# Written order on ScalarE and VectorE, and the product G2-G3 moved behind M7, in a two-layer GLA and retention trunk

## The chip, the cores and the metric

The kernel runs on one core of a Trainium2 chip. The metric is the device time of one execution in microseconds (us). The median of three runs stands for a kernel; one execution is also recorded by the hardware profiler, and all rows below come from that one.

A core has five engines, each with its own instruction queue worked off in order: TensorE (PE; matmuls, its weight loads are listed as PEld), ScalarE (ACT), VectorE (DVE), GpSimd (POOL) and SyncE (SP, which here only issues transfers). Sixteen DMA engines move data between HBM and the on-chip memory SBUF; matmuls write to PSUM.

## What is computed

The reference is a decoder trunk of two layers on 256 tokens of width 2048, in float32: one layer of gated linear attention (GLA, 4 heads) and one of retention (8 heads), each with RMSNorm before it, a SiLU gate, an output projection and a residual add, and a last RMSNorm.

```python
def gla_mixer(h, w_in, ...):           # retention_mixer has the same frame
    q, k, v, gate = split(h @ w_in)    # k-dimension 2048
    o = chunked_attention(q, k, v, decay)
    return (norm(o) * silu(gate)) @ w_out

for i in range(2):
    h = h + mixer_i(rms_norm(h, g_i))
return rms_norm(h, final_norm)
```

Nearly all the work is the products with `w_in` and `w_out`, all in float32 accuracy: every float32 block is split into a high part `hi` (rounded to what the fast matmul format holds) and a rest `lo`, and three matmuls (high with high, high with low, low with high) stand for one.

## The kernel before, in words

**Blocks.** The weights are cut into blocks of 256 rows of the k-dimension by 512 columns. A block lies in SBUF as a tile of 128 partitions by 1024 numbers (512 KB), which holds two k-tiles. A group of 512 output columns takes 8 blocks. `_plan` (L56) writes two lists: `loads`, the blocks to be fetched in order, and `subs`, the blocks to be split in order (576 of them).

**Split.** `emit_split` (L226) takes the next entry of `subs`: ScalarE copies the block to `hi` (L238), VectorE subtracts to get `lo` (L239). `hi` and `lo` have 4 buffers each, plain blocks (`raw`) 4 as well. `next_weights` (L263) keeps the splits 3 entries ahead of the one that TensorE is about to use (`LOOK = 3`); plain loads are issued from the SP queue 3 loads ahead of the splits (`DMA_LOOK = 3`).

**A pair.** `pair` (L310) makes one group of value columns V and one group of gate columns G together, 16 times in all: 8 times in the GLA layer (tile names `ga_...`) and 8 times in the retention layer (`re_...`). Blocks G4 to G7 and V4 to V7 are used plainly (`normal`, L338: 12 matmuls, both token halves). For blocks 0 to 3 of both, a 2x2 scheme of Winograd's kind takes 7 products where 8 would be needed (`product`, L330: two blocks, 12 matmuls of 512 columns over one token half or over a sum of halves). Its weight sums are formed in place: after a block G0, G1, V2 or V3 was split, GpSimd issues a transfer that adds the next block to it in SBUF (L245, `accum_op=ALU.add`), and the sum is split again. In this document G0' is the block G0 after the first addition (G0+V0), G0'' after the second (+V2), G0''' after the third (+G2); G1 goes with it, and V2', V3' are V2+V0 and V3+V1. So each of G0 and G1 passes a chain of three rounds: split, transfer, split, transfer, split, transfer, split.

**Order of TensorE in a pair, before.** G0-G1 | V4 | V2-V3 | V5 | G0'-G1' | V6 | G2-G3 | first half of V7 | G0''-G1'' | second half of V7 | V2'-V3' (this product is called M7) | G4 | G0'''-G1''' | G5 | G6 | G7. This order is fixed on TensorE: `wmm` stamps each matmul with one token, and instructions of one engine that carry it keep their written order. On ScalarE and VectorE there was no such stamp: a scheduler orders them by priority (written order, unless `high_priority` lifts an instruction) and by its own simulated times.

**Copies and joins.** The 7 products share PSUM banks, so intermediate sums are copied out by ScalarE (`keepf`, L358 to L360): `sg[0]` from bank g1 after G0-G1, `o[1]` from bank g0 after G0'-G1', `o[0]` from g1 after G0''-G1'', and `sg[1]` from g1 after M7. The next matmul that writes the bank waits for the copy. After M7, the next one that writes g1 is the second half of G4: 6 matmuls lie between. VectorE joins the pieces (L389 to L393, L402), `v_split` (L656) scales and splits V, and `g_silu` (L667) applies SiLU at the end of the pair.

**Beside the pairs.** Small steps of attention (`side`) are advanced one after each product or block: rotation, scores, decay, transposes. Each head begins with a group of query and key columns (`group_w`, 8 blocks), and after every 2 GLA heads or 4 retention heads comes a half of the output projection (`out_half`).

Of the kernel before, what the change touches and what calls it, by code (L numbers as in the profile page):

```python
# [10 lines left out]
F32 = mybir.dt.float32  # L11
# [3 lines left out]
AF = mybir.ActivationFunctionType  # L15
ALU = mybir.AluOpType
# [39 lines left out]
def _plan():  # L56


    loads, subs, last = [], [], {}

    def load(gid, j, tag="raw"):
        last[gid, j] = len(loads)
        loads.append((gid, j, tag))

    def use(gid, js, add=None):
        for j in js:
            subs.append((last[gid, j], None if add is None else (add[0], add[1] + j % 2)))

    def plain(gid, js=range(NSUB)):
        for j in js:  # L70
            load(gid, j, "xz"[j // 2] if not subs and j < 4 else "raw")
            use(gid, [j])

    def pair(g, v):
        def fresh(gid, js, tag="raw"):
            for j in js:
                load(gid, j, tag)
            use(gid, js)

        fresh(g, (0, 1), "x")  # L80
        fresh(v, (4,))
        fresh(v, (2, 3), "z")
        fresh(v, (5,))
        use(g, (0, 1), (v, 0))
        fresh(v, (6,))
        fresh(g, (2, 3))
        fresh(v, (7,))
        use(g, (0, 1), (v, 2))
        use(v, (2, 3), (v, 0))
        fresh(g, (4,))  # L90
        use(g, (0, 1), (g, 2))
        fresh(g, (5,))
        fresh(g, (6,))
        fresh(g, (7,))

    def gla(h):
        plain(("aqk", h))
        for g in (2 * h, 2 * h + 1):
            pair(("ag", g), ("av", g))

    def ret(h):
        plain(("rqk", h))
        pair(("rg", h), ("rv", h))

    def out_half(name, half):
        cut = READY[name]
        for js in (range(cut), range(cut, NSUB)):
            for c in range(2):
                plain((name, half, c), js)
        for c in (2, 3):  # L110
            plain((name, half, c))

    for half in range(2):
        for h in (2 * half, 2 * half + 1):
            gla(h)
# [13 lines left out]
def kernel(  # L129
# [17 lines left out]
    nc = tc.nc  # L147
# [19 lines left out]
    mm = nc.tensor.matmul  # L167
    keep = tc.keep_in_program_order

    def wmm(*args, **kw):  # L170
        tc.stamp_issue_order_token(nc.tensor.matmul(*args, **kw).ins, "weights")  # L171


    def const(shape, name, dtype=F32):
# [51 lines left out]
    def emit_split(pieces=1):  # L226
        i = emitted["sub"]
        if i >= len(subs):
            return
        c = subs[i][0]  # L230
        while emitted["raw"] <= min(c + DMA_LOOK, len(loads) - 1):
            emit_raw()
        src = raws[c]
        hi, lo = split_tiles(i)
        step = SUB // pieces
        for k in range(pieces):
            sl = slice(k * step, (k + 1) * step)
            nc.scalar.activation(hi[:, sl], src[:, sl], AF.Copy)  # L238
            nc.vector.tensor_tensor(lo[:, sl], src[:, sl], hi[:, sl].bitcast(F32), ALU.subtract)  # L239
        splits[i] = (hi, lo)  # L240
        emitted["sub"] += 1
        later[c].popleft()
        if later[c]:
            more = w_all[places[later[c][0]]].rearrange("p (k n) -> p k n", n=GW)
            nc.gpsimd.dma_start(src, more, accum_op=ALU.add)  # L245
# [64 lines left out]
    def pair(lhs, name, on_v, on_g, hook):  # L310
# [3 lines left out]
        v = v_p.tile([P, 2, 2, GW], F32R, tag="v", name=f"{name}_v")  # L314
        sg = sg_p.tile([P, 2, GW], F32, tag="sg", name=f"{name}_sg")
        o = o_p.tile([P, 2, GW], F32, tag="o", name=f"{name}_o")
        g1, v0, v1, g0 = acc(4, f"{name}_ps")
# [12 lines left out]
        def product(ps, left, stop=False):  # L330
            for j in range(2):
                hi, lo = next_weights()
                for q in range(SUB):
                    k = j * SUB + q
                    three(ps, left(k, 0), left(k, 1), hi, lo, q, stop and k == QK - 1)
            advance()

        def normal(p0, p1, j, stop=False, halves=False):  # L338
            hi, lo = next_weights()

            def half(t):
                for q in range(SUB):
                    kt = j * SUB + q
                    cols = slice(t * P, (t + 1) * P)
                    three((p0, p1)[t], lhs[:, kt, 0, cols], lhs[:, kt, 1, cols], hi, lo, q, stop and q == SUB - 1)
                if t:
                    advance()

            half(0)
            if halves:  # L350
                return lambda: half(1)
            half(1)

        plain = lambda kt0, t: lambda k, a: lhs[:, kt0 + k, a, t * P : (t + 1) * P]
        summed = lambda i: lambda k, a: s[:, i, k, a, :]
        tt = nc.vector.tensor_tensor

        def keepf(dst, ps):  # L358
            with tc.high_priority():
                nc.scalar.activation(dst, ps, AF.Copy)  # L360

        product(g1, plain(0, 0), stop=True)
        keepf(sg[:, 0, :], g1)
# [2 lines left out]
        hook(1)  # L366
        product(v0, summed(0))
        hook(2)
        normal(v0, v1, 5)
        hook(3)  # L370
        product(g0, summed(1), stop=True)
        keepf(o[:, 1, :], g0)
        begun.discard(id(g0))
        closed.discard(id(g0))
        hook(4)
        normal(v0, v1, 6)
        hook(5)
        product(g0, plain(4, 0))
        hook(6)
        second = normal(v0, v1, 7, stop=True, halves=True)  # L380
        product(g1, summed(2), stop=True)
        keepf(o[:, 0, :], g1)
        second()
        product(g1, summed(3), stop=True)
        keepf(sg[:, 1, :], g1)
        hook(7)
        normal(g0, g1, 4)
        hook(8)
# [9 lines left out]
        normal(g0, g1, 6)  # L398
        hook(11)
        normal(g0, g1, 7, stop=True)  # L400
        with tc.high_priority():
            tt(sg[:, 0, :], g0, sg[:, 0, :], ALU.add)  # L402
            on_g(sg, [sg[:, 0, :], g1])
        return sg

    def make_sums(lhs, name):
# [249 lines left out]
    def v_split(r2):  # L656
        def run(v, o):
            for t in range(2):
                x, sc = o[:, t, :], r2[:, t : t + 1]
                nc.scalar.activation(v[:, t, 0, :], x, AF.Copy, scale=sc)  # L660
                nc.vector.scalar_tensor_tensor(
                    v[:, t, 1, :], x, sc, v[:, t, 0, :].bitcast(F32), ALU.mult, ALU.subtract
                )

        return run

    def g_silu(r):  # L667
        def run(sg, src):
            for t in range(2):
                keep(nc.scalar.activation(sg[:, t, :], src[t], AF.Silu, scale=r[:, t : t + 1]))  # L670

        return run

# [585 lines left out]
```

## Time and profile before

| What | Value |
|---|---|
| Median of 3 runs | 1492.73 us (1484.79 to 1494.83) |
| The profiled execution | 1495.53 us |
| Its span, first to last instruction | 1493.8 us |
| TensorE busy | 1423.0 us (95%), 6608 matmuls |
| VectorE busy | 1063.3 us (71%) |
| ScalarE busy | 844.1 us (57%) |
| GpSimd busy | 175.2 us (12%) |
| TensorE clock granted, mean | 0.978 of full speed |
| DMA | 340.21 MB, mean 228 GB/s |

How to read the rows: in the list of waits a row names the waiting engine, the tile and line of its instruction, after the arrow who ended the wait, then the total in us, the number of waits and the longest. In a timeline a row has the start and the length in us, engine, line, operation, tiles as out<-in with their shapes, and in brackets the idle time of the engine before it and what ended it. In a table of stretches each engine has its busy time with the number of instructions; then come the granted share of the TensorE clock, the DMA engines' mean busy share and GB/s. An x count in a table of one line counts that line's instructions alone. A matmul's length overlaps the next one's; what counts is the distance of their starts.

### The profile page before, as it was taken

What the parts mean: (1) busy time and instruction counts of PE and PEld (TensorE: products, weight loads), DVE (VectorE), ACT (ScalarE), POOL (GpSimd) and SP (SyncE); (2) the same over time, 40 slices, a digit from 0 to 9 for tenths busy, and PEclk for the clock granted to TensorE, in tenths of its full rate; (3) what the DMA queues carried; (4) which work ended last, traced back from release to release, by engine and by line L of the source; (5) the groups of instructions that cost most, each with busy time, mean ns of one, the idle gap of its engine ahead of it and who ended that gap; (6) DMA issues with size and microseconds to landing.
All of it is one profiled execution on the core that took longest, in us unless ns stands there. A gap on an engine that the chain in (4) does not pass through costs nothing. (4 is left out here: it accounts for less than half of the span.)

```text
span 1493.8 us, 18563 instructions
## 1 busy us (share of the span) xinstructions
PE 1423.0 (95%) x6608; PEld 1160.4 (78%) x6608; DVE 1063.3 (71%) x1602; ACT 844.1 (57%) x1135; POOL 175.2 (12%) x237
## 2 busy tenths in 40 slices
PE   8898998999998999999999899989999999999997
PEld 6677876888876878788878787868888777787887
DVE  8689688854896696666767777766547676768664
ACT  4676675653575566554656565654335555656553
POOL 1111213000140032000111111110002010101000
PEclk9999998999999999999999999999999999999999
DMA  9997699556989689755996969696579697969663
GB/s 314 307 237 223 163 257 250 204 187 197 291 241 259 169 233 226 278 172 181 280 270 172 268 173 275 170 318 194 187 256 269 218 233 219 249 191 234 236 199 111
DMA packets 90332, 340.21 MB, mean 228 GB/s; under 512 B 10416, under 2 KB 10928, under 8 KB 88832
## 3 DMA queue, kind: packets, MB, share of 16 engines
q1 hardware_dynamic: 67344, 240.81, 46.7%
q0 software_dynamic: 22176, 97.14, 30.2%
q8 instruction: 52, 0.85, 0.2%
q10 hardware_dynamic: 720, 1.09, 0.2%
q14 instruction: 40, 0.33, 0.1%
HBM read 326.41 MB, written 12.58 MB: 227 GB/s over the span
## 5 line engine op out<-in xcount | busy, mean ns | idle before, releaser
L239 DVE TENSOR_TENSOR lo<-raw_raw,hi 128x1024 fp32r<-128x1024 f32 x375 | 459.4, 1228 | 241.4 <-ACT hi L238 238.6
L238 ACT ACTIVATE hi<-raw_raw 128x1024 fp32r<-128x1024 f32 x375 | 396.0, 1057 | 359.9 <-PE ga_ps L171 76.0
L171 PE MATMUL re_ps<-hi,xhl 128*128 128x512 f32 x704 | 236.6, 407 | 24.9 <-ACT re_sg L360 24.9
L171 PE MATMUL ga_ps<-hi,xhl 128*128 128x512 f32 x704 | 240.2, 412 | 15.5 <-ACT ga_sg L360 13.0
L238 ACT ACTIVATE hi<-raw_x 128x1024 fp32r<-128x1024 f32 (+1 forms) x130 | 136.0, 1052 | 166.5 <-DMA raw_x<-in_w_all 98.2
L239 DVE TENSOR_TENSOR lo<-raw_x,hi 128x1024 fp32r<-128x1024 f32 (+1 forms) x130 | 157.0, 1217 | 101.0 <-ACT hi L238 98.2
L171 PEld LDWEIGHTS re_ps<-hi,xhl 128*128 128x128 f32 x704 | 137.1, 195 | 60.3 <-ACT re_sg L360 28.4
L171 PE MATMUL rqk_ps<-xhl,hi 128*128 128x512 f32 x512 | 179.7, 393 | 1.5 <-ACT re_sg L670 1.5
L171 PEld LDWEIGHTS ga_ps<-hi,xhl 128*128 128x128 f32 x704 | 138.6, 197 | 51.9 <-ACT ga_sg L360 16.4
L171 PE MATMUL ga_ps<-lo,xhl 128*128 128x512 f32 x352 | 146.1, 415 | 2.8 <-DVE lo L239 2.6
L171 PE MATMUL re_ps<-lo,xhl 128*128 128x512 f32 x352 | 143.3, 407 | 0.0
L171 PE MATMUL rqk_ps<-xhl,lo 128*128 128x256 f32 x512 | 140.3, 283 | 0.0
L245 POOL DMA_DIRECT2D raw_x<-in_w_all x96 | 83.3, 868 | 347.9 <-DVE lo L239 315.2
L171 PEld LDWEIGHTS rqk_ps<-xhl,hi 128*128 128x128 f32 x512 | 94.9, 188 | 21.4 <-ACT re_sg L670 3.4
L171 PEld LDWEIGHTS rqk_ps<-xhl,lo 128*128 128x128 f32 x512 | 96.7, 189 | 2.5
L171 PE MATMUL gqk_ps<-xhl,hi 128*128 128x512 f32 x256 | 92.3, 402 | 0.8 <-ACT ga_sg L670 0.6
L171 PE MATMUL ga_ps<-hi,sums_a 128*128 128x512 f32 x256 | 85.9, 394 | 1.4 <-ACT ga_o L360 0.9
L171 PEld LDWEIGHTS ga_ps<-lo,xhl 128*128 128x128 f32 x352 | 69.5, 197 | 22.2 <-DVE lo L239 6.7
L171 PE MATMUL re_ps<-hi,sums_r 128*128 128x512 f32 x256 | 85.2, 392 | 0.3 <-ACT hi L238 0.2
L239 DVE TENSOR_TENSOR lo<-raw_z,hi 128x1024 fp32r<-128x1024 f32 x64 | 77.2, 1223 | 9.2 <-ACT hi L238 9.0
L171 PE MATMUL gb_ps<-hi,ogt 128*128 128x512 f32 x256 | 81.9, 397 | 0.0
L171 PE MATMUL ra_ps<-hi,ogt 128*128 128x512 f32 x256 | 81.0, 396 | 0.0
(297 smaller groups left out, 2271.9 us busy)
## 6 DMA issues: line engine op xcount, KB each, us to landing
raw_raw<-in_w_all SPq DMA_DIRECT2D x383, 512.0 KB, 4.4
raw_x<-in_w_all POOLq DMA_DIRECT2D x96, 512.0 KB, 7.3
raw_x<-in_w_all SPq DMA_DIRECT2D x32, 512.0 KB, 4.7
raw_z<-in_w_all SPq DMA_DIRECT2D x32, 512.0 KB, 7.2
raw_z<-in_w_all POOLq DMA_DIRECT2D x32, 512.0 KB, 5.8
xn<-in_x_n SPq DMA_DIRECT2D x4, 512.0 KB, 9.4
sums_a_kept<-sums_a POOLq DMA_DIRECT2D x1, 2048.0 KB, 11.3
gg<-in_gn_g POOLq DMA_DIRECT2D x8, 256.0 KB, 3.9
```

The source lines that it names most:

```text
L171: tc.stamp_issue_order_token(nc.tensor.matmul(*args, **kw).ins, "weights")
L238: nc.scalar.activation(hi[:, sl], src[:, sl], AF.Copy)
L239: nc.vector.tensor_tensor(lo[:, sl], src[:, sl], hi[:, sl].bitcast(F32), ALU.subtract)
L245: nc.gpsimd.dma_start(src, more, accum_op=ALU.add)
```

## The change

Three things are done.

1. In a pair, V5 goes behind G0'-G1', and the product G2-G3 goes behind M7, so that the new order is: G0-G1 | V4 | V2-V3 | G0'-G1' | V5 | V6 | first half of V7 | G0''-G1'' | second half of V7 | V2'-V3' (M7) | G2-G3 | G4 | G0'''-G1''' | G5 | G6 | G7. `_plan` lists loads and splits in the same order. The numbers of loads, splits, additions and matmuls stay.
2. The splits, the copies `keepf`, the joins, `v_split` and `g_silu` carry the same token as the matmuls (`queued`, `wact`, `wtt`), so that among themselves they keep their written order on ScalarE and on VectorE.
3. `high_priority` is taken off `keepf` and off the last join with its SiLU.

```diff
-        fresh(v, (5,))
         use(g, (0, 1), (v, 0))
-        fresh(v, (6,))
-        fresh(g, (2, 3))
-        fresh(v, (7,))
+        for j in (5, 6, 7):
+            fresh(v, (j,))
         use(g, (0, 1), (v, 2))
         use(v, (2, 3), (v, 0))
+        fresh(g, (2, 3))
         fresh(g, (4,))
...
+    def queued(ins):
+        tc.stamp_issue_order_token(ins.ins, "weights")
+        return ins
+
     def wmm(*args, **kw):
-        tc.stamp_issue_order_token(nc.tensor.matmul(*args, **kw).ins, "weights")
+        queued(nc.tensor.matmul(*args, **kw))
+
+    def wact(*args, **kw):
+        return queued(nc.scalar.activation(*args, **kw))
+
+    def wtt(*args):
+        queued(nc.vector.tensor_tensor(*args))
...
-            nc.scalar.activation(hi[:, sl], src[:, sl], AF.Copy)
-            nc.vector.tensor_tensor(lo[:, sl], src[:, sl], hi[:, sl].bitcast(F32), ALU.subtract)
+            wact(hi[:, sl], src[:, sl], AF.Copy)
+            wtt(lo[:, sl], src[:, sl], hi[:, sl].bitcast(F32), ALU.subtract)
...
-        tt = nc.vector.tensor_tensor
+        tt = wtt
 
         def keepf(dst, ps):
-            with tc.high_priority():
-                nc.scalar.activation(dst, ps, AF.Copy)
+            wact(dst, ps, AF.Copy)
...
-        normal(v0, v1, 5)
-        hook(3)
         product(g0, summed(1), stop=True)
         keepf(o[:, 1, :], g0)
         begun.discard(id(g0))
         closed.discard(id(g0))
+        hook(3)
+        normal(v0, v1, 5)
         hook(4)
         normal(v0, v1, 6)
         hook(5)
-        product(g0, plain(4, 0))
-        hook(6)
         second = normal(v0, v1, 7, stop=True, halves=True)
         product(g1, summed(2), stop=True)
         keepf(o[:, 0, :], g1)
         second()
         product(g1, summed(3), stop=True)
         keepf(sg[:, 1, :], g1)
+        hook(6)
+        product(g0, plain(4, 0))
         hook(7)
         normal(g0, g1, 4)
...
-        with tc.high_priority():
-            tt(sg[:, 0, :], g0, sg[:, 0, :], ALU.add)
-            on_g(sg, [sg[:, 0, :], g1])
+        tt(sg[:, 0, :], g0, sg[:, 0, :], ALU.add)
+        on_g(sg, [sg[:, 0, :], g1])
```

In `v_split` and `g_silu` the same three calls are wrapped in `wact` and `queued`.

More of the change, by code (lines that the diff above doesn't have):

```diff
@@ L659, in run @@
                 x, sc = o[:, t, :], r2[:, t : t + 1]
-                nc.scalar.activation(v[:, t, 0, :], x, AF.Copy, scale=sc)
-                nc.vector.scalar_tensor_tensor(
-                    v[:, t, 1, :], x, sc, v[:, t, 0, :].bitcast(F32), ALU.mult, ALU.subtract
+                wact(v[:, t, 0, :], x, AF.Copy, scale=sc)
+                queued(
+                    nc.vector.scalar_tensor_tensor(
+                        v[:, t, 1, :], x, sc, v[:, t, 0, :].bitcast(F32), ALU.mult, ALU.subtract
+                    )
                 )
@@ L669, in run @@
             for t in range(2):
-                keep(nc.scalar.activation(sg[:, t, :], src[t], AF.Silu, scale=r[:, t : t + 1]))
+                keep(wact(sg[:, t, :], src[t], AF.Silu, scale=r[:, t : t + 1]))
         return run
```

## The prediction

> **What bounds the kernel now.** The page first, for the busy shares, then the list of waits of TensorE alone.
>
> ```profile
> PE 1423.0 (95%) x6608; PEld 1160.4 (78%) x6608; DVE 1063.3 (71%) x1602; ACT 844.1 (57%) x1135; POOL 175.2 (12%) x237
> ```
> ```profile
> PE re_ps L171 <- ACT re_sg L360: 24.9, 8, 5.3
> PE ga_ps L171 <- ACT ga_sg L360: 13.0, 6, 3.5
> PE ga_ps L171 <- DVE lo L239: 6.3, 10, 0.9
> ...
> PE re_ps L171 <- DVE lo L239: 2.9, 6, 0.8
> ```
>
> TensorE is the bound. What can be won is its idle time, and most of that has one cause: 24.9 + 13.0 = 37.9 us, in 14 of 16 pairs, ended by the copy at L360 into `sg`. The copy in question is that of `sg[1]` after M7. One pair (first matmul at 887) shows how it comes to be late. First TensorE, then ScalarE.
>
> ```profile
> 887.05 0.40 PE L171 MATMUL re_ps<-hi,xhl 128*128 128x512 f32 x1
> ...
> 909.28 0.39 PE L171 MATMUL re_ps<-hi,sums_r 128*128 128x512 f32 x1
> 909.51 0.39 PE L171 MATMUL re_ps<-lo,sums_r 128*128 128x512 f32 x1
> ...
> 912.19 0.50 PE L171 MATMUL re_ps<-lo,sums_r 128*128 128x512 f32 x1 [0.76 <-DVE lo L239]
> ...
> 918.72 0.40 PE L171 MATMUL re_ps<-hi,xhl 128*128 128x512 f32 x1
> 921.32 0.50 PE L171 MATMUL re_ps<-hi,xhl 128*128 128x512 f32 x1 [2.20 <-ACT re_sg L360]
> ```
> ```profile
> 909.81 1.06 ACT L238 ACTIVATE hi<-raw_x 128x1024 fp32r<-128x1024 f32 x1 [3.02 <-DMA raw_x<-in_w_all]
> 910.78 1.99 ACT L238 ACTIVATE hi<-raw_z 128x1024 fp32r<-128x1024 f32 x2
> 913.63 0.60 ACT L360 ACTIVATE re_o<-re_ps 128x512 f32<-128x512 f32 x1 [0.86 <-PE re_ps L171]
> 914.13 1.06 ACT L238 ACTIVATE hi<-raw_raw 128x1024 fp32r<-128x1024 f32 x1
> ...
> 919.11 1.06 ACT L238 ACTIVATE hi<-raw_x 128x1024 fp32r<-128x1024 f32 x1 [2.12 <-DMA raw_x<-in_w_all]
> 920.08 0.71 ACT L660 ACTIVATE re_v<-re_o,r 128x512 fp32r<-128x512 f32 x1
> 920.69 0.57 ACT L360 ACTIVATE re_sg<-re_ps 128x512 f32<-128x512 f32 x1
> ```
>
> Matmuls start 0.23 us apart (909.28 to 909.51), so a whole product or block of 12 takes 2.8 us and a half 1.4. From 909.28 on come G0''-G1'', half of V7, M7; after 918.72 the second half of G4 wants bank g1. The copy that frees it starts only at 920.69, because ScalarE stands at the split of G1''' (919.11), which waits 2.12 us for its addition, and then does a piece of `v_split`. So the wait is a place in ScalarE's queue, behind a transfer that TensorE does not need yet.
>
> The idle time isn't all of it. The next table takes line 171 alone, in 13 stretches of 10 us, each from where such a wait begins.
>
> ```profile
> 72.40:82.40 10.00, 7.36 (x20) 0.68 0.85 285
> 123.70:133.70 10.00, 6.43 (x19) 0.83 0.61 211
> 473.40:483.40 10.00, 6.51 (x21) 0.83 0.78 274
> 551.80:561.80 10.00, 7.24 (x19) 0.66 0.79 271
> 601.30:611.30 10.00, 7.68 (x27) 0.83 1.02 423
> 769.00:779.00 10.00, 7.22 (x25) 0.83 0.75 258
> 843.00:853.00 10.00, 6.31 (x21) 0.83 0.73 282
> 918.70:928.70 10.00, 7.80 (x27) 0.83 0.85 300
> 991.60:1001.60 10.00, 4.75 (x13) 0.66 1.01 418
> 1156.90:1166.90 10.00, 6.97 (x24) 0.83 0.88 309
> 1231.30:1241.30 10.00, 7.41 (x32) 1.00 0.86 288
> 1302.90:1312.90 10.00, 6.04 (x19) 0.83 0.79 291
> 1378.00:1388.00 10.00, 8.59 (x37) 1.00 0.89 328
> ```
>
> In 11 of the 13 the granted clock is below full: 0.83 is 1.7 us of full-speed work lost out of 10. The stretch at 918.70 has it after an idle time of 2.20 us. All 13 hold 304 matmuls, 70 us of work at 0.23, in 130 us: 60 us are lost. Some of it is side work in two of the stretches; I take **58 us**, 38 of waiting and 20 of slow clock.
>
> [...]
>
> **The change part by part.** Its sum is made against the profiled execution: 1495.53 us, span 1493.8, so 1.7 lie outside. That execution is 2.8 us above the median of the runs, 1492.73, which I leave as noise.
>
> *G2-G3 behind M7.* Now 12 + 6 matmuls, 4.2 us, lie between the end of M7 and the next write to g1, where there were 6 (1.4). Written order puts three splits ahead of the copy, those of G2, G3 and G4: plain blocks, loaded long before, whose buffers come free one by one up to the middle of M7. The last split takes 1.06, the copy 0.60; both fit into 4.2 with 2.5 to spare. G0''' and G1''' come behind the copy. So the wait goes: **-58**, with 0 to -60 as its ends (nothing if something else in ScalarE's queue takes the split's place). What is late next is the chain of additions, below.
>
> *Order of the chain.* The three gaps of G0 from use to use were, in units of 2.8 us, 4, 3.5 and 3.5; now 3, 3.5 and 4.5. The sum stays, the last gap (where G1''' was late) wins 2.8 us, and the first loses them. These rows price the first two rounds.
>
> ```profile
> 880.68 1.06 ACT L238 ACTIVATE hi<-raw_x 128x1024 fp32r<-128x1024 f32 x1 [1.71 <-PE rqk_ps L171]
> ```
> ```profile
> 883.33 0.88 POOL L245 DMA_DIRECT2D raw_x<-in_w_all  x1 [1.43 <-DVE lo L239]
> 898.39 0.86 POOL L245 DMA_DIRECT2D raw_x<-in_w_all  x1 [0.28 <-DVE lo L239]
> ```
> ```profile
> DMA to landing us min/median/max: 5.3/7.1/11.9
> ```
> ```profile
> 884.00:896.00 12.00, 12.00 (x62) 1.00 0.69 150
> 896.00:908.00 12.00, 12.00 (x57) 1.00 1.01 237
> ```
> ```profile
> q1 hardware_dynamic: 67344, 240.81, 46.7%
> ...
> L239 DVE TENSOR_TENSOR lo<-raw_raw,hi 128x1024 fp32r<-128x1024 f32 x375 | 459.4, 1228 | 241.4 <-ACT hi L238 238.6
> ```
>
> First round, G1: split at 880.68, addition issued at 883.33, landed at 890.4 with the median of L245 and at 895.2 with the longest. G1' is used 3.5 units after 887.05 (G0, G1, V4, V2-V3, then G0'), at 896.9, and must be split from 894.7 on (1.06 + 1.23, less the matmul that needs only `hi`). At the median 4 us are left over, at the longest 0.5 is missing. Ends 0 and +8 over 16 pairs; I take **+2**, near the median.
>
> Second round, G1'': now the addition is issued at 898.39 and landed just ahead of 909.81, 11.3 us; its `lo` is due at 910.9 and TensorE gets it at 912.19, 1.3 late. After the change its use is one product earlier, `lo` due at 908.1. Its addition goes out one subtraction (1.23) earlier, as V5's now comes behind; with the same 11.3 it lands at 908.5 and `lo` is done at 910.8: 2.7 late. Against that: the DMA engines are full from 896 on (1.01) and not before (0.69). The written order of loads moves V7's ahead of that stretch, since it now follows V6 and finds its buffer earlier, and those of G6 and G7 behind it, since they now wait for the splits of G2 and G3. One plain load takes 46.7% x 1493.8 / 459 = 1.5 us of all engines (240.81 MB are 459 blocks of 0.524 MB), so two to three of them are 3 us or more: 0 late. In the mean over the pairs the wait for `lo` is now (6.3 + 2.9) / 16 = 0.6 us. Ends: -9 and +22 (16 x 1.4). I take half a us more per pair, **+8**.
>
> *Copy of `o[0]`.* Written order now puts G2's split ahead of it; so far the copy came first (913.63, then 914.13). It must be done in the 1.4 us of V7's second half; the split takes 0.97 till the next may start (909.81 to 910.78), the copy 0.60, a sum of 1.6 with semaphores 1.7: 0.3 late per pair, **+5**. Ends 0 and +28 (rival 3).
>
> *Last join and SiLU without priority.* Behind them waits the first matmul of the next group on that bank. At most one ScalarE instruction like that of 0.71 comes ahead: 0 to +11, I take **+4**. The stamp as such adds no instruction. Loads, additions and splits stay 459 on SP, 128 on POOL, 576 on both engines; POOL's order of additions stays. `v_split` now comes after the split that follows G7; nobody reads V before the next head's end of scores, so nothing waits. The other copies (`sg[0]`, `o[1]`) have the same splits ahead as before or plain ones, and their banks are written again several products later: 0.
>
> [...]
>
> Sum: -58 + 2 + 8 + 5 + 4 = -39; 1495.5 - 39 = 1456.5, and I forecast **1456 us**. Its own range is 1440 (all 58 and no new wait) to 1472 (the new waits doubled).
>
> **The rivals.**
>
> 1. *The second round becomes late and takes the clock along.* G1'' 2.7 us late in every pair: +14 over my sum; an idle time above 2.2 us drew the slow clock in the row at 918.70, so 1.7 more in half or all pairs, +14 to +27: 1484 to 1497. For it: DMA share 1.01 to 1.04 around this place. Against: three loads leave it.
> 2. *Slower: the additions become the bound.* If the first round, now right behind the additions of V2 and V3, takes the longest 11.9 instead of 7.1, G1' is split 0.6 late and G1'' 3.4: 16 x (3.4 - 1.1) = 37, and the clock falls each time, 27: 1456 + 64 = 1520. [...] Against: in that stretch (884 to 896) the engines are busy 0.69 of the time only.
> 3. *The copy of `o[0]` waits for V7.* If the scheduler gives G2's `hi` the buffer of V7 rather than that of G1'', split and copy start only after V7's second half: 1.7 us per pair, 28 instead of 5: 1479. Against: at 914.13 the third split after G1'' began before V7's second half was done, so it had another buffer.
> 4. *The wait stays.* Something else holds the copy after M7 (side work on ScalarE, a late load of G4): 1495, or a little less.
>
> **How the numbers follow.** My forecast 0.63, better than 1440 0.06, rival 1 0.11, rival 2 0.08, rival 3 0.07, rival 4 0.05. About 1% is what a measurement of this kernel can tell from no change, so faster is below 1478 and slower above 1507. Faster: 0.69 and half of rival 3, 0.73; slower: rival 2 and something unforeseen, 0.11; the rest 0.16. The range goes from 1440 to 1490: it leaves out the better case, rivals 2 and 4 and the upper end of rival 1.
>
> **What will show it.** Right: no wait of TensorE for `sg` at L360 over 1 us, fewer stretches with half clock (a mean near 0.99), the copy after M7 starting within 0.2 us of M7's end, G0''' split without waiting for its addition. New small waits on `lo` (G1'') and on the copy into `o`. Wrong: waits for `lo` of over 2 us, or for `o` of 1.7, with the clock falling behind them; or additions that land over 12 us after their issue.

## The result, and the profile after

The kernel after took 1493.15 us in the median of 19 runs (1486.57 to 1501.84), the kernel before, on the same chips, 1493.12 (19 runs). The ratio is 1.0006, with a 95% interval of 0.9988 to 1.0023: no difference that can be measured, where 1456 us (1440 to 1490) was forecast. The profiled execution has a span of 1489.2 us against 1493.8. Of all executions reported below one, of the kernel *before_hold*, took 3548 us, far from every other, and the ratio of that kernel leaves it out.

First the page of the kernel after: the busy time of each engine.

```profile
PE 1421.6 (95%) x6608; PEld 1153.1 (77%) x6608; DVE 1062.2 (71%) x1602; ACT 839.5 (56%) x1133; POOL 183.2 (12%) x237
```

Nothing was saved or added in work; 1423.0 us of TensorE became 1421.6. Next, the waits of TensorE in the kernel after (total in us, times, longest).

```profile
PE ga_ps L174 <- DVE lo L180: 17.6, 25, 1.9
PE ga_ps L174 <- ACT hi L177: 8.5, 6, 2.5
PE re_ps L174 <- ACT hi L177: 8.5, 8, 1.2
PE re_ps L174 <- DVE lo L180: 8.1, 12, 0.8
...
PE ga_ps L174 <- ACT ga_o L177: 2.1, 5, 1.0
...
PE re_ps L174 <- ACT re_o L177: 0.9, 4, 0.2
```

The two rows that headed this list before, 24.9 and 13.0 us of waiting for the copy into `sg`, are gone; no wait for that copy is left. In their place stand waits for splits: `lo` and `hi` together 42.7 us in these four rows. All waits of TensorE in this list add up to 62.0 us before and 58.8 after. So the change did what it says, and the time came back as another wait of nearly the same size.

The waits are of two kinds. The first is seen in the pair that answers to the one at 887 before; its first matmul is at 890 here. TensorE around G1'', then ScalarE, then POOL, from the timeline of the kernel after.

```profile
910.76 0.39 PE L174 MATMUL re_ps<-hi,sums_r 128*128 128x512 f32 x1
912.26 0.50 PE L174 MATMUL re_ps<-hi,sums_r 128*128 128x512 f32 x1 [1.11 <-ACT hi L177]
913.52 0.50 PE L174 MATMUL re_ps<-lo,sums_r 128*128 128x512 f32 x1 [0.76 <-DVE lo L180]
```
```profile
911.15 1.06 ACT L177 ACTIVATE hi<-raw_x 128x1024 fp32r<-128x1024 f32 x1 [2.83 <-PE re_ps L174]
...
919.65 0.60 ACT L177 ACTIVATE re_sg<-re_ps 128x512 f32<-128x512 f32 x1 [0.33 <-PE re_ps L174]
920.15 2.00 ACT L177 ACTIVATE hi<-raw_x 128x1024 fp32r<-128x1024 f32 x2
```
```profile
897.53 0.86 POOL L254 DMA_DIRECT2D raw_z<-in_w_all  x1 [1.54 <-DVE lo L180]
899.42 1.83 POOL L254 DMA_DIRECT2D raw_x<-in_w_all  x2 [1.04 <-DVE lo L180]
```

The copy into `re_sg` starts as its product ends (ScalarE had been idle for 0.33 us), and the splits of G0''' and G1''' (920.15, one right behind the other) wait for nothing: the middle of the change works as planned. But the split of G1'' starts at 911.15, and TensorE stands twice for it, 912.26 - 910.76 - 0.23 = 1.27 us for `hi` and 1.03 for `lo`. Before, it stood once, for `lo`. The row at 911.15 names a matmul as what ended ScalarE's wait, because one ended at that moment; what it waited for is the addition. The trace has its landing at 911.04, and in all 16 pairs the split of G1'' starts 0.08 to 0.11 us after that landing, also where no matmul ends there. Such stands come in every retention pair: the waits at G0'' and G1'' are 16.6 us in these eight pairs, against 3.2 before.

The second kind is on ScalarE. These rows of its waits, in the kernel after, were 1.1, 1.5 and 1.5 us before.

```profile
ACT re_sg L177 <- DVE re_sg L180: 15.6, 8, 2.4
ACT ga_v L177 <- DVE ga_o L180: 14.1, 7, 4.1
...
ACT ga_sg L177 <- DVE ga_sg L180: 13.1, 6, 4.5
```

They are the pinned SiLU and the pinned `v_split`, each waiting at the head of ScalarE's queue for a join on VectorE: 42.8 us. The experiments take these two kinds apart.

### The profile page after: what moved, and what is told of

It is laid out like the page before. It is cut to its first block, busy times and chain, and to the rows that moved or that the text cites. A ratio compares the mean times of both kernels' runs of the same rounds, so it can differ in the third digit from the quotient of the medians.

```text
span 1489.2 us, 18573 instructions
## 1 busy us (share of the span) xinstructions
PE 1421.6 (95%) x6608; PEld 1153.1 (77%) x6608; DVE 1062.2 (71%) x1602; ACT 839.5 (56%) x1133; POOL 183.2 (12%) x237
## 4 chain that ended last, share of the span: by engine, by line
PE 30%; issue 21%; DMA 5%; ACT 2%; DVE 2%; POOL 1%; POOLq 0%; ACTq 0%
PE re_ps L174 12%; PE ra_ps L174 6%; PE rb_ps L174 5%; PE rqk_ps L174 4%; DMA raw_x<-in_w_all 4%; PE tail_ps L174 2%; DVE lo L180 1%; ACT hi L177 1%; DMA gb_resid<-ga_sum 1%; POOL raw_x L254 1%; POOL raw_z L254 1%; DMA raw_raw<-in_w_all 1%; PE ga_ps L174 0%; PE rot_tp L702 0%; PE ro_ps L693 0%
## 5 line engine op out<-in xcount | busy, mean ns | idle before, releaser
L174 PE MATMUL ga_ps<-hi,xhl 128*128 128x512 f32 x704 | 229.4, 400 | 3.8 <-ACT qk L488 2.2
L174 PE MATMUL re_ps<-hi,xhl 128*128 128x512 f32 x704 | 229.3, 400 | 0.0
L174 PE MATMUL rqk_ps<-xhl,hi 128*128 128x512 f32 x512 | 178.8, 392 | 0.0
L174 PEld LDWEIGHTS ga_ps<-hi,xhl 128*128 128x128 f32 x704 | 134.0, 190 | 36.1 <-ACT qk L488 2.5
L174 PEld LDWEIGHTS re_ps<-hi,xhl 128*128 128x128 f32 x704 | 134.3, 191 | 31.8
L174 PE MATMUL ga_ps<-lo,xhl 128*128 128x512 f32 x352 | 142.5, 405 | 8.4 <-DVE lo L180 8.4
L174 PE MATMUL re_ps<-lo,xhl 128*128 128x512 f32 x352 | 140.8, 400 | 0.0
L174 PE MATMUL rqk_ps<-xhl,lo 128*128 128x256 f32 x512 | 140.3, 283 | 0.0
L174 PEld LDWEIGHTS rqk_ps<-xhl,hi 128*128 128x128 f32 x512 | 94.9, 188 | 18.2
L174 PE MATMUL re_ps<-hi,sums_r 128*128 128x512 f32 x256 | 89.6, 411 | 9.4 <-ACT hi L177 8.5
L174 PEld LDWEIGHTS rqk_ps<-xhl,lo 128*128 128x128 f32 x512 | 96.7, 189 | 2.5
L174 PE MATMUL ga_ps<-hi,sums_a 128*128 128x512 f32 x256 | 88.7, 410 | 9.1 <-ACT hi L177 7.0
L174 PE MATMUL gqk_ps<-xhl,hi 128*128 128x512 f32 x256 | 91.5, 399 | 1.1 <-ACT hi L177 1.1
L174 PEld LDWEIGHTS ga_ps<-lo,xhl 128*128 128x128 f32 x352 | 67.0, 190 | 28.9 <-DVE lo L180 13.6
L174 PE MATMUL gb_ps<-hi,ogt 128*128 128x512 f32 x256 | 81.8, 397 | 0.0
L174 PE MATMUL ra_ps<-hi,ogt 128*128 128x512 f32 x256 | 81.3, 396 | 0.0
## 6 DMA issues: line engine op xcount, KB each, us to landing
sums_a_kept<-sums_a POOLq DMA_DIRECT2D x1, 2048.0 KB, 11.3
```

The source lines that it names most:

```text
L174: queued(nc.tensor.matmul(*args, **kw))
```

## The experiments

The theory after reading the trace had two parts. **Theory T**: the new order of blocks makes the second round of sums, G1'', late, and that gives back part of the gain. **Theory P**: the pins on `v_split` and on the SiLU make ScalarE stand in front of ready splits, and that gives back the rest (the expectations of the first two runs call this second part Theory S). The rivals: the additions as such have become the bound; or the lost priority on the last join is what costs. All ratios are to executions of the kernel before beside the same runs (their medians lie between 1491.32 and 1493.67), with 95% intervals; spans, clocks and rows are those of one profiled execution each.

| run | median us | ratio | span | clock |
|---|---|---|---|---|
| before | 1493.12 | | 1493.8 | 0.978 |
| after | 1493.15 | 1.0006 [0.9988, 1.0023] | 1489.2 | 0.984 |
| pin_only | 1481.88 | 0.9930 [0.9906, 0.9955] | 1479.4 | 0.990 |
| order_only | 1471.04 | 0.9876 [0.9843, 0.9910] | 1469.7 | 0.990 |
| no_add | 1434.44 | 0.9624 [0.9598, 0.9649] | 1430.0 | 0.996 |
| unread | 1496.31 | 1.0048 [1.0023, 1.0072] | 1497.8 | 0.977 |
| free_tail | 1475.33 | 0.9874 [0.9850, 0.9899] | 1474.3 | 0.990 |
| order_defer | 1514.21 | 1.0133 [1.0105, 1.0160] | 1512.2 | 0.970 |
| old_copy_first | 1465.35 | 0.9806 [0.9782, 0.9831] | 1462.3 | 0.990 |
| v5_copy_first | 1478.89 | 0.9903 [0.9872, 0.9933] | 1482.3 | 0.989 |
| prio_back | 1489.01 | 0.9982 [0.9963, 1.0000] | 1488.5 | 0.986 |
| vsplit_free | 1473.26 | 0.9863 [0.9840, 0.9887] | 1470.4 | 0.988 |
| silu_free | 1472.00 | 0.9859 [0.9838, 0.9880] | 1470.9 | 0.990 |
| before_hold | 1490.24 | 0.9992 [0.9975, 1.0009] | 1492.2 | 0.981 |

### The two halves of the change, each alone

*pin_only* is the kernel after with the old order of blocks; *order_only* is the kernel before with the new order, its priorities kept and nothing pinned.

The first against the kernel after:

```diff
+        fresh(v, (5,))
         use(g, (0, 1), (v, 0))
-        for j in (5, 6, 7):
-            fresh(v, (j,))
+        fresh(v, (6,))
+        fresh(g, (2, 3))
+        fresh(v, (7,))
...
-        fresh(g, (2, 3))
...
+        normal(v0, v1, 5)
+        hook(3)
         product(g0, summed(1), stop=True)
...
+        product(g0, plain(4, 0))
+        hook(6)
         second = normal(v0, v1, 7, stop=True, halves=True)
...
-        hook(6)
-        product(g0, plain(4, 0))
```

> The kernel after with the block order of before: only the pins and the lost priorities are left of the change. Theory T (the second additions of G0 and G1 land too late in the new block order, and TensorE waits for G1'' instead of the copy): the pins are neutral, 1493 us within 8, with the wait for the copy into sg after M7 as in the kernel before (over 20 us in all), because the written order also puts the splits of G4, G0''' and G1''' ahead of that copy. Theory S (the pins keep ScalarE and VectorE waiting and eat what the order wins): 1515 us or more.

> The kernel before with the new block order alone, no pins, priorities kept. Theory T: 1493 us within 8, TensorE waiting 1 to 2.5 us for hi and lo of G1'' in most pairs, no wait for sg. Theory S: about 1460 us, as the order alone wins its 30 us and more.

Measured: 0.9930 for the pins and 0.9876 for the order. Each alone is faster, and together they are not: 1481.88 and 1471.04 us against 1493.15. Neither theory had expected that: T had both at 1493 within 8, S had 1515 or more for the pins and about 1460 for the order. The waits of TensorE, first of pin_only, then of order_only.

```profile
PE re_ps L175 <- ACT re_sg L178: 17.2, 8, 3.9
...
PE ga_ps L175 <- ACT ga_sg L178: 5.3, 5, 2.2
```
```profile
PE ga_ps L170 <- DVE lo L238: 11.6, 17, 2.2
PE re_ps L170 <- ACT hi L237: 9.0, 8, 1.3
PE re_ps L170 <- DVE lo L238: 8.1, 11, 0.8
PE ga_ps L170 <- ACT hi L237: 4.0, 4, 2.2
```

In the old order the pins shorten the wait for `sg` (22.5 instead of 37.9 us), since a pinned `v_split` can no longer slip in ahead of the copy; that piece took 0.61 us in the pair at 887, so it explains some 10 of the 15 us at most. The split that waits for its addition still stands ahead of the copy. The new order needs no pin to lose that wait. But it already has the waits for G1'': `lo` and `hi` come to 32.7 us in its four rows, where `lo` was 9.2 before. Sorted by place in the pair, the waits at G0'' and G1'' are 22.4 us (17.0 of them in the retention pairs), against 6.6 before. That is Theory T, and it holds without a pin. Most of the rest stands in the GLA pairs, ahead of G1' (3.2), V5 (3.0) and G2-G3 (3.7).

The sum can be closed with the time from one matmul start to the next, less the median for that width (0.232 us at 512 columns, 0.118 at 256, 0.109 at 128), added up over the whole trace. It is 108.1 us before, 84.0 in order_only and 103.5 after, so 24.1 and 4.6 less; the spans differ by 24.1 and 4.6 us too. Of it, 25.9, 10.9 and 22.4 us lie in stretches with half clock (a granted share of 0.50, as over 923 to 925 before and over 986 to 989 after). So the order alone won 15.0 us of clock and 9.1 of waiting, and the pins on top of it lost 11.5 and 8.0. The share of the clock is that of these executions: prio_back below, with every pin, has nearly the time of the kernel after and 17.0 us in half clock.

### What the additions cost

Both kernels are the kernel after with its order and pins. *no_add* leaves the 128 additions out, so the sums of weight blocks aren't computed and their products come from other data; *unread* keeps the additions, but the splits of the sums read a constant, so what is computed from the sums is left out.

```diff
-            nc.gpsimd.dma_start(src, more, accum_op=ALU.add)
+            pass
```
```diff
-            wact(hi[:, sl], src[:, sl], AF.Copy)
-            wtt(lo[:, sl], src[:, sl], hi[:, sl].bitcast(F32), ALU.subtract)
+            if subs[i][1] is None:
+                wact(hi[:, sl], src[:, sl], AF.Copy)
...
+            else:
...
+                wact(eight(hi), still, AF.Copy)
+                wtt(eight(lo), still, eight(hi).bitcast(F32), ALU.subtract)
```

> The kernel after without the 128 additions (the sums are left out: each split reads the block as first loaded). It takes away the wait and the traffic. Theory T: no faster than with additions that nobody reads by more than 5 us, about 1455 us. Rival B: clearly faster than that one, by 15 us or more.

> The kernel after, with all 128 additions running as before, but the splits of G0', G0'', G0''', V2' and so on read a constant instead of the sum, so that nobody waits for an addition (what is computed from the sums is left out). Theory T: the waits for hi and lo of G0'' and G1'' go, and the slow clock behind them, about 1455 us. Rival B (the DMA engines are simply full and give no more blocks per time): the waits move to plain blocks, 1480 us or more.

Without the additions 1434.44 us, 58.7 less than after. Of the waits for `hi` only 0.5 us is left, of those for `lo` 9.3, and the mean clock is 0.996. So 58.7 us is what the additions cost the kernel after, wait and traffic together, and Theory T points at the right transfers. With the additions running unread, 1496.31 us: both runs came out as Rival B had expected, not as Theory T had. The second tells less than was meant: the splits of the sums no longer held the additions back. POOL's waits before those to G blocks ended 57 times with the landing of a transfer into such a block (162.8 us; in the kernel after once, 8.8 us), so they could run early, into the plain loads.

```profile
ACT hi L177 <- DMA raw_raw<-in_w_all: 95.7, 40, 5.6
```

That row, ScalarE waiting for a plain load, is 19.3 us in the kernel after. The additions cost the same 60 us, while the plain loads came late. What it shows is that here the additions made the plain loads late even when nobody waited for them; it doesn't show what the splits' waiting costs by itself, and is inconclusive on Theory T.

### Undoing the pins on the tail

*free_tail* is the kernel after with the pins kept on splits, copies and joins, taken off `v_split` and the SiLU, and the priority put back around the last join and SiLU.

```diff
-                wact(v[:, t, 0, :], x, AF.Copy, scale=sc)
+                nc.scalar.activation(v[:, t, 0, :], x, AF.Copy, scale=sc)
...
-                keep(wact(sg[:, t, :], src[t], AF.Silu, scale=r[:, t : t + 1]))
+                keep(nc.scalar.activation(sg[:, t, :], src[t], AF.Silu, scale=r[:, t : t + 1]))
...
+        with tc.high_priority():
             tt(sg[:, 0, :], g0, sg[:, 0, :], ALU.add)
```

> The kernel after with the pins kept on splits, copies and joins, but taken off v_split and g_silu, and with the priority back on the last join and SiLU. Theory P (pinned, these ScalarE instructions stand in front of the joins that they read, and the next splits, which are ready, stand behind them: waits of ScalarE for joins of 43 us in the kernel after, none such with the order alone): as fast as the order alone, 1471 us within 6, V2's split of each second GLA pair 5 us ahead of its use instead of 1 to 3. Rival Q (the pins on the splits and copies themselves cost, as the copy of o[0] behind G2's split): 1485 us or more.

0.9874, the ratio of order_only (0.9876). All that the pins lost on the new order lies in these three edits, as Theory P expected; the pins on splits, copies and joins cost nothing there that can be measured. The next three kernels split the edit: the priority alone, `v_split` alone, the SiLU (with the priority) alone.

> The kernel after, with the priority back around the last join and the SiLU behind it, and every pin kept. Theory P (what costs is ScalarE standing, in an order that is now fixed, at `v_split` and at the SiLU ahead of splits that are ready): the order of the pinned instructions stays, so ScalarE still stands in front of the subtractions and joins of VectorE as before this edit (re_sg 15.6, ga_v 14.1, ga_sg 13.1 us); ratio to before 0.995 to 1.003. Rival (the priority is what was lost: the last join waits on VectorE behind side work): most of the 18 to 20 us that the freed tail won come back, 1475 to 1480 us, ratio 0.988 to 0.992.

> The kernel after, with `v_split` alone taken out of the pinned order (both its instructions); the SiLU stays pinned and without priority. Theory P: the wait of ScalarE in front of the joins of `o` in the GLA pairs (ga_v 14.1 us, longest 4.1) goes, that in front of the SiLU (re_sg 15.6, ga_sg 13.1) stays; by the share of these waits in 46.5 us a third of the 18 to 20 us comes back, about 1487 us, ratio 0.994 to 0.998. If the `v_split` is the whole of it: 1475, ratio 0.988.

> The kernel after, with the SiLU alone taken out of the pinned order and the priority back around it and the last join; `v_split` stays pinned. Theory P: the waits in front of the SiLU (re_sg 15.6, ga_sg 13.1 us) go, that of ga_v (14.1) stays; by their share two thirds of the 18 to 20 us come back, about 1481 us, ratio 0.990 to 0.994. If the SiLU is the whole of it: 1475, ratio 0.988. If `v_split` is: 1493.

The priority: 0.9982 against 1.0006 for the kernel after, with intervals that overlap, so it isn't what was lost. The other two fell outside what Theory P expected: **freeing either one brings the whole back** (0.9863 and 0.9859), not a third and two thirds. (silu_free has the priority back as well, which alone is worth 0.2% at the middle of its interval.) And the standing of ScalarE itself is no measure of the loss. First its waits in vsplit_free, then in silu_free.

```profile
ACT re_sg L177 <- DVE re_sg L180: 15.4, 8, 2.2
...
ACT ga_sg L177 <- DVE ga_sg L180: 13.5, 7, 2.7
```
```profile
ACT ga_v L177 <- DVE ga_o L180: 13.3, 6, 3.7
```

In vsplit_free ScalarE stands before the SiLU for 28.9 us, as in the kernel after (28.7), and it costs nothing that can be measured; in silu_free it stands before `v_split` for 13.3, and that costs nothing either. In pin_only and no_add all three stands are there, 41.8 us in each, and both are faster than the kernel after. What differs are TensorE's waits in the GLA pairs alone. In vsplit_free, then in silu_free:

```profile
PE ga_ps L174 <- DVE lo L180: 9.7, 13, 1.9
...
PE ga_ps L174 <- ACT hi L177: 6.0, 7, 2.2
```
```profile
PE ga_ps L174 <- DVE lo L180: 10.9, 15, 1.9
...
PE ga_ps L174 <- ACT hi L177: 2.7, 3, 1.1
```

`ga_ps` waits 26.1 us for `lo` and `hi` in the kernel after, and 15.7 and 13.6 here (15.6 in order_only). `re_ps` waits 16.6 us in the kernel after and 14.9 and 16.3 here. So the pins cost in the GLA pairs and nothing in the retention pairs. The spans say the same: the first matmul of the retention layer starts at 721.1 us in the kernel after and at 704.4 in order_only, 704.2 in vsplit_free and 701.8 in silu_free, and from there to the end it takes 768.1, 765.3, 766.2 and 769.1. One GLA pair, the second of its head, shows how. ScalarE in the kernel after, then in silu_free:

```profile
449.88 0.72 ACT L177 ACTIVATE ga_v<-ga_o,rr 128x512 fp32r<-128x512 f32 x1 [3.31 <-DVE ga_o L180]
450.51 1.04 ACT L177 ACTIVATE hi<-raw_x 128x1024 fp32r<-128x1024 f32 x1
...
455.81 0.69 ACT L870 ACTIVATE ga_o<-go_ps,rr 128x512 f32<-128x512 f32 x1 [3.31 <-PE go_ps L693]
456.52 1.28 ACT L177 ACT_TABLE_LOAD   x1
457.81 0.72 ACT L177 ACTIVATE ga_sg<-ga_sg,rr 128x512 f32<-128x512 f32 x1
...
459.01 1.99 ACT L177 ACTIVATE hi<-raw_z 128x1024 fp32r<-128x1024 f32 x2
```
```profile
437.12 0.72 ACT L177 ACTIVATE ga_v<-ga_o,rr 128x512 fp32r<-128x512 f32 x1 [3.31 <-DVE ga_o L180]
...
439.65 2.17 ACT L177 ACTIVATE hi<-raw_z 128x1024 fp32r<-128x1024 f32 x2
```

With the SiLU free, V2 and V3 are split 2.5 us after the second piece of `v_split`. With it pinned the order is `v_split`, G0 and G1, SiLU, V2 and V3, and they are split 9.1 us after it: the fixed order leaves a gap, a free piece of output work falls into it and waits there (3.31 us), then comes the load of the SiLU's table (1.28 us). V2's and V3's additions go out that much later, and the second round's right behind them. POOL in the kernel after, then in silu_free:

```profile
461.78 1.82 POOL L254 DMA_DIRECT2D raw_z<-in_w_all  x2 [6.74 <-DVE lo L180]
463.99 0.87 POOL L254 DMA_DIRECT2D raw_x<-in_w_all  x1 [0.39 <-DVE lo L180]
```
```profile
444.40 0.86 POOL L254 DMA_DIRECT2D raw_z<-in_w_all  x1 [2.11 <-DVE lo L180]
```

They go out 11.9 us after the second piece of `v_split` in one and 7.3 in the other. TensorE then stands for G1'' at 477.65 (1.19 us for `hi`) and 478.91 (0.76 for `lo`) in the kernel after, and not at all in this pair of silu_free. The other pairs agree. This is when the addition to V2 goes out, in us after the pair's first matmul:

| | second GLA pair of heads 1 to 4 | all eight retention pairs |
|---|---|---|
| after | 7.0, 16.4, 9.9, 7.7 | 4.9 |
| order_only | 3.0, 4.5, 5.2, 3.8 | 4.9 |
| vsplit_free | 4.2, 7.2, 5.0, 7.2 | 4.9 |
| silu_free | 4.0, 7.1, 5.2, 5.4 | 4.9 |

In a retention pair there is no such pile, whatever is pinned. That either one is enough to win the time back is measured, and that the pile shrinks with it is seen in the table (in vsplit_free not in the last head). That the pile is all of the 20 us is not shown: in these four pairs TensorE waits at G0'' and G1'' for 8.8 us in the kernel after and 4.3, 5.9 and 2.2 in the other three, and the rest of the waits is spread over other places.

### Can the second round be had in time?

*order_defer* takes order_only and issues the additions of V2 and V3 behind those of G0' and G1', so that the second round of sums has the DMA engines earlier.

```diff
-            nc.gpsimd.dma_start(src, more, accum_op=ALU.add)
+            held.append((src, more)) if loads[c][2] == "z" else add_on(src, more)
+        if loads[c][1:] == (1, "x"):
+            while held:
+                add_on(*held.popleft())
```

> The order alone, with the additions to V2 and V3 issued behind those to G0' and G1' (a token on GpSimd keeps that order), where they went ahead of them. Theory C (G1'' is late because its addition shares the DMA engines with those of V2 and V3, which nobody needs for another 10 us): the wait for hi and lo of G1'' falls from 2.3 us per pair to under 1, and the slow clock with it, about 1455 us. Rival (the plain loads fill the engines, or the additions to G0' and G1' one another): within 5 us of the order alone, 1471.

```profile
PE re_ps L170 <- ACT re_o L367: 34.3, 8, 5.2
PE ga_ps L170 <- ACT ga_o L367: 24.0, 8, 4.0
```

These are TensorE's waits in order_defer. The wait for G1'' is gone (no row for `hi` in the pairs, 4.2 + 1.5 us for `lo`): it was the additions of V2 and V3 ahead of it that made it late, as Theory C had it. The time of 1455 us that Theory C gave is missed by 59, because now V2' and V3' are late, ScalarE stands at their splits (78.8 us for `raw_z`), and behind them in its queue stands the copy into `o[0]`: 58.3 us of waiting, slower than before by 1.3%. It is the same kind of wait as the one that was removed, at another copy.

*old_copy_first* keeps the old order of blocks, in which G1'' has its time, with the free tail, and instead holds back the look-ahead: during M7 no split beyond that of G4 is written, so that the pinned copy into `sg[1]` stands ahead of those of G0''' and G1'''. *v5_copy_first* does the same with V5 alone moved behind G0'-G1'.

```diff
-        product(g1, summed(3), stop=True)
+        product(g1, summed(3), stop=True, upto=2)
...
-                hi, lo = next_weights()
+                hi, lo = next_weights(LOOK if upto is None else upto - j)
```

> The block order of before, pins on splits, copies and joins, v_split and SiLU free, and the splits' lead is held back at M7, so that the copy of sg[1] stands ahead of the splits of G0''' and G1'''. If the copy's place in ScalarE's queue was the whole trouble and the block order need not change: the waits for sg go to under 5 us, G1'' waits 0.6 us per pair as before, about 1450 us, faster than the order alone. If the waits only move (G0''' and G1''' then late for their product): 1475 us or more.

> As the run with the copy first, with V5 alone moved behind G0'-G1': the gaps of the chain are 3, 4.5 and 3.5 units instead of 4, 3.5 and 3.5. If the second round is the tight one (12 to 15 us from split to landing against 9 for the first): no wait for G1'' is left, 5 to 10 us faster than the run with the copy first, about 1443 us. If the first round with its 3 units becomes the tight one: waits for G1', slower than that run.

```profile
PE ga_ps L175 <- DVE lo L181: 11.3, 14, 2.0
PE re_ps L175 <- DVE lo L181: 4.9, 8, 0.8
```

These are the waits in old_copy_first, the fastest that computes everything: 1465.35 us, 0.9806 [0.9782, 0.9831], faster than both kernels, though not the 1450 that was expected. There is no wait for the copy into `sg`, and in the retention pairs TensorE waits 5.8 us for `lo` and `hi` where it is 17.1 in order_only; in the GLA pairs it is 14.9, hardly less than the 15.6 there. What removes the `sg` wait is thus the place of two splits in ScalarE's queue; the move of blocks isn't needed for it, and brings the lateness of G1'' in the retention pairs with it. The old order with these pins and the free tail but without the held look-ahead was not run, so the 1.9% belong to the three together. v5_copy_first, halfway between, ends at 0.9903, slower than old_copy_first where 5 to 10 us less were expected. At G0'' and G1'' 0.6 us of waiting are left, as expected, but TensorE now stands ahead of G0''' (7.4 us in the retention pairs, 2.3 in old_copy_first) and V7 (3.6, and none there), and ScalarE waits 117.2 us for plain loads instead of 47.3. Which of these costs how much stays open.

The last run asks whether that one edit is enough without any pin: *before_hold* is the kernel before with the held look-ahead alone, the same lines as above.

> The kernel before, with its old order of blocks, no pins and its priorities, and one edit: during M7 no split is written beyond that of G4, so that those of G0''' and G1''' come behind the copy into sg[1]. Loads and additions are issued in the same order as before. Theory (a split that waits for its addition stood ahead of that copy, and this is the whole of the wait): TensorE waits for sg go from 40 to under 4 us, its half-clock loss from 26 to about 11, G1'' stays at lo 10 to 16 us and hi under 5: 1460 to 1470 us, ratio 0.978 to 0.985. Rival (the pins are needed for it, or hold what the other run of this look-ahead won): the copy still stands behind a v_split or a plain split, 1475 to 1485, ratio 0.988 to 0.995.

```profile
PE re_ps L171 <- ACT re_sg L360: 22.1, 8, 4.6
PE ga_ps L171 <- ACT ga_sg L360: 17.3, 7, 4.7
```

0.9992: nothing. The wait for `sg` is still there, 39.4 us. ScalarE in before_hold shows why.

```profile
917.16 1.06 ACT L238 ACTIVATE hi<-raw_x 128x1024 fp32r<-128x1024 f32 x1 [2.24 <-DMA raw_x<-in_w_all]
918.12 0.71 ACT L660 ACTIVATE re_v<-re_o,r 128x512 fp32r<-128x512 f32 x1
918.73 0.57 ACT L360 ACTIVATE re_sg<-re_ps 128x512 f32<-128x512 f32 x1
```

The split of G1''' (and 3 us earlier that of G0''') and a piece of `v_split` stand ahead of the copy, although both splits are now written behind it and the copy has priority. Without the pin, written order isn't the order of the queue: the theory was wrong and the rival right in mechanism, while its 1475 to 1485 us were too few. For the old order of blocks the pins are needed; the priority doesn't do it.

## Why the prediction was wrong

Step by step, as the prediction had them:

- **The wait for the copy into `sg[1]`, -58 (38 of waiting, 20 of clock).** Right in mechanism. In order_only the 37.9 us are gone to the last row, and half clock fell from 25.9 to 10.9 us, 15 of the 20. In the kernel after the clock won only 3.5.
- **First round, G0' and G1', +2.** Right: in order_only TensorE stands there for 3.2 us, all of it in GLA pairs, where it was 0.9 before; in the kernel after it is 2.6.
- **Second round, G1'', +8 (ends -9 and +22).** Mis-sized, and the first step that failed. The waits at G0'' and G1'' rose from 6.6 us before to 22.4 in order_only, by 16 where 8 was forecast. All waits for `lo` and `hi` rose from 11.5 to 34.7, by 23; the other 7 are mostly the GLA pairs' waits ahead of G1', V5 and G2-G3, of which the sum has only the +2. What failed is that three plain loads leave the full stretch, worth 3 us or more. SyncE's issues, before and after, from the same place of the two pairs (start, time until the last, count):

```profile
885.80 19.26 SPq L205 DMA_DIRECT2D raw_raw<-in_w_all  x6
```
```profile
888.97 15.84 SPq L214 DMA_DIRECT2D raw_raw<-in_w_all  x4
```

  Two loads did leave: one by one in the trace, five plain loads are under way while the addition that makes G1'' runs in the pair before, and three in the pair after. But that addition, the second of the two issued at 899.42, goes out some 0.9 us later and lands at 911.04, 10.6 us after that. Before it was issued at 898.39 and landed at 909.43, 11.0 us. The relief was 0.4 us, not 3, and in the mean of the eight retention pairs there was none: 10.7 us from issue to landing before, 11.2 in the kernel after, 11.3 in order_only. What it stands behind are the additions of V2 and V3, issued last at 897.53: with those two behind it, in order_defer, it took 8.5 us in the mean, and in this pair 910.18 - 901.56 = 8.6 to the split.

```profile
901.56 0.85 POOL L252 DMA_DIRECT2D raw_x<-in_w_all  x1 [0.28 <-DVE lo L238]
```
```profile
910.18 1.06 ACT L237 ACTIVATE hi<-raw_x 128x1024 fp32r<-128x1024 f32 x1 [2.98 <-DMA raw_x<-in_w_all]
```

  The prediction had rival 1 for this, G1'' late by 2.7 us in every pair, with the chance of 0.11; in the retention pairs it is what happened, at 1.27 + 1.03 = 2.3 us in the pair shown. Its price was too low by the prediction's own rows: it counts 1.4 us more per pair, from the 1.3 of one pair, but the mean wait before was 0.6, so 2.7 in every pair would be 34 us and not 22. That the measured 1493 lies in rival 1's 1484 to 1497 is luck: the late G1'' alone, in order_only, gave 1471.
- **Copy of `o[0]` behind G2's split, +5.** Right: 2.1 + 0.9 = 3.0 us in the rows of the kernel after, 0.24 us at 916.57 in the pair shown there against 0.3 forecast. Rival 3 didn't come.
- **Last join and SiLU without priority, +4; `v_split` pinned, 0.** Here is the second failed step. The +4 for the priority fits: prio_back is 0.24% below the kernel after, 3.6 us, not clear of the noise. But "nobody reads V before the next head's end of scores, so nothing waits" looked only at who reads V, and not at who stands behind `v_split` on ScalarE; and for the SiLU the prediction counted what comes ahead of it, not the splits behind it. On the new order the two pins cost 24.1 - 4.6 = 19.5 us of span (order_only against after), and with either one freed nothing that can be measured is left of it. The prediction weighed standing in ScalarE's order for the copies, that into `o[0]` above all, and not for these splits. In the rows at 449.88 to 459.01 it is the splits of V2 and V3 that stand behind the pinned pieces, 9.1 us after the second piece of `v_split` where it is 2.5 us with the SiLU free.
- **The clock.** The prediction took its slow clock behind a late G1'' (rival 1) from the one row at 918.70, a stand of 2.20 us. No run shows that length as a threshold: stands of 1.3 and 1.0 us close together brought half clock in one pair (a granted share of 0.72 over 840 to 846) and not in another (1.00 over 912 to 918; more in the last section).

The sum: -58 + 2 + 8 + 5 + 4 forecast -39, and the spans differ by -4.6. The part of the order, -58 + 2 + 8 = -48, measured -24.1: the waits for `lo` and `hi` rose by 13 us more than forecast, the clock won 5 less, other waits cost 1, and some 4 us I have not located. The part of the pins and the lost priority, +5 + 4 = +9, measured +19.5.

## What to carry to other kernels

An instruction that is pinned into an engine's order is to be priced by what stands behind it, not by who reads its result (here two splits, 9.1 us after the second piece of `v_split` instead of 2.5); and two kinds of pins that each cost nothing can cost together, here where they fell into one stretch of a pair (0.9863 and 0.9859 with one of them, 1.0006 with both). Where a wait comes from the place of two instructions in a queue, move those two (with a pin, since without one the written order needn't be the order of the queue) before moving the work around them: here that was worth 1.9%, the larger rearrangement 1.2% alone and nothing with all its pins. And with the DMA engines nearly full (a busy share of 1.01, 1.05 and 0.99 in three stretches of 6 us from 896.6 on in the kernel after), the sum that was used one product earlier, G1'', was late by 2.3 us in the pair shown, and putting its addition first, in order_defer, made V2' and V3' late (58.3 us of TensorE's waiting for the copy behind their splits).

## What the hardware showed that I had not expected

- Two waits of ScalarE of the same kind and 28.9 and 13.3 us in total cost no measurable time alone; together they cost 19.5 us, 11.5 of it as half clock on TensorE in the executions compared.
- Half clock after nearly the same stand came in one pair and not in the next. Two stretches of the kernel after, each behind the stand for G1'' (matmuls at L174 alone; us and busy times, then granted clock, DMA share and GB/s):

```profile
912.00:918.00 6.00, 4.75 (x18) 3.38 (x19) 1.00 0.95 183
...
984.00:990.00 6.00, 5.17 (x12) 3.75 (x13) 0.53 0.95 175
```

  Ahead of the first lie stands of 1.27 and 1.03 us, ahead of the second 1.30 and 1.03, and 0.54 at G0'' before them. That third stand doesn't decide it: in the pair whose G1'' starts at 839.95, stands of 1.31 and 1.03 us alone brought half clock (0.72 over 840 to 846), and in the one at 1147.80, stands of 0.73, 1.30 and 1.03 brought none (1.00 over 1146 to 1152). What decides between them stays open.
- The additions are dear where the DMA engines are full (the shares of 0.99 to 1.05 above): those for G1'' take 11.2 us from issue to landing in the mean of the retention pairs of the kernel after, against a median of 7.2 us over all of its additions to G blocks. All 128 together cost 58.7 us (no_add against after), 0.46 us each, and 61.9 when nobody waited for their data (unread against no_add).
